# Moving the fetches of the returning tiles and the bias loads in the queue of an attention stage

## The chip, the cores and the metric

The kernel runs on one core of one Trainium2 chip. The metric is the device time of one launch in microseconds. The time before is the median of three runs, 2206.3 us (2204.29 to 2207.11). Engines are called as in the profile: PE (matrix), DVE (vector), ACT (scalar), POOL (GpSimd), SP (the engine that here only issues DMAs); PEld is the loading of PE's stationary operand.

## The reference

One layer of a decoder on 512 tokens of width 2048: RMSNorm, an attention mixer with 16 heads of width 128 in 4 key/value groups, a residual add, RMSNorm, a SwiGLU FFN with 5632 hidden columns, a residual add and a last RMSNorm. The mixer has three branches, and their outputs are added with gates computed from the tokens:

```python
s_c = q . kcc + bias_c          # 31 compressed key blocks
s_s = q . ks  + bias_s          # selected blocks; with 512 tokens all 8 blocks are selected
s_w = q . kw  + bias_w          # sliding window of 512
o = gates[0] * softmax(s_c) @ vcc + gates[1] * softmax(s_s) @ vs + gates[2] * softmax(s_w) @ vw
h = x + o @ w_out
```

Each softmax is causal, and the bias depends on the distance of query and key. Everything is float32.

## The kernel before, in words

Matmuls are done three times on split operands: a float32 matrix is kept as a high part (rounded) and a low part (the rest), and `three` adds high x high, high x low and low x high in PSUM (L267, L268 and L269). Splitting costs one ACT instruction (the high part) and one DVE instruction (the low part): for weights these are L97 and L98, which turn a loaded `raw` tile into `whi` and `wlo`.

The attention stage runs over heads `h`, and for each head over four blocks `t` of 128 queries (block `t` sees `t + 1` blocks of keys). The parts of its work:

- `scores(h, t)`: PE computes the scores of all three branches into one PSUM tile `sc`; DVE adds the bias (`tb`, one tile of 128 x 512 a head, in a pool of two) and finds the maximum (L791); ACT takes exponentials and their sums (L793) into the tile `P[t]`. `P[0]` and `P[2]` share memory, and so do `P[1]` and `P[3]`.
- `finish(h, t)`: DVE scales by gate over sum (L798, L799, L805) and transposes within blocks of 32 x 32 (L806); then SP issues four DMAs that write `P[t]` to DRAM, `d_p[t]` (L808). This is the way out of a tile.
- `fetch(t)`: SP issues one DMA that reads `d_p[t]` back into its place in the tile `PT` (L812, `ptr<-d_p`). With the blocks placed anew, this completes the transpose. There is one place for each `t`, so it can be written again only when the last reader of the head before is done. This is a returning tile.
- `turn(h, b, kt)`: ACT and DVE split the part of `PT` that key block `kt` of branch `b` needs (L829 and L833, into `pth` and `ptl`). The order is `kt` = 3, 2, 1, 0, each for branch 0 and 1, and last the compressed branch (`b` = -1), in which DVE writes low parts with L831. Key block 3 needs tile 3 alone, key block 2 needs tiles 2 and 3, and so on. The compressed branch reads all four places and is their last reader.
- `values(h, b, kt)`: PE multiplies with the values and adds in the PSUM tile `o` (L267 to L269; L844 for the compressed branch). `head_out` splits `o`; for heads below 12 two DMAs write it to DRAM (L855).

The order is written out by hand. A head has 12 steps. In step `i`, `turn` does part `i` and `values` does part `i - 2`; in between stand the scores of the next head (steps 2, 5, 8 and 11 for `t` = 3, 2, 1, 0) and their `finish` (steps 3, 6 and 9 for `t` = 3, 2 and 1, and step 0 of the next head for `t` = 0). After each step `pump` gives PE matmuls of other work (the projections of later heads and groups, and at the end a part of the output projection), until a running sum has reached the step's share of 20800 per head. The weights of that work are loaded by POOL (`W.queue = pool`).

All of these `L808`, `L812`, `L855` and bias DMAs are issued by SP, in program order: an issue that has to wait holds back all behind it. In heads 12 to 15 SP also issues `reload_o` (three pairs of 1 MB each from `d_o` into `hn_h` and `hn_l`, L696), and transfers of the tile `stage` (L702, L718).

The functions that the diff touches:

Of the kernel before, what the change touches and what calls it, by code (L numbers as in the profile page):

```python
# [19 lines left out]
S, D, H, DH, G, HPG = 512, 2048, 16, 128, 4, 4  # L20
# [153 lines left out]
def nsa_block(ctx: ExitStack, tc: tile.TileContext, x, rel_bias, mix_g, ffn_g, fin_g, w_in, w_out,  # L174
# [455 lines left out]
    with ExitStack() as st2:  # L630
# [105 lines left out]
        def pump(h, step):  # L736
            at = h + (step + 4) / STEPS
            goal = 20800 * min(at, 13) + 18300 * max(at - 13, 0)
            while done["ns"] < goal:
                c = next(stream, "end")  # L740
                if c == "end":
                    return
                done["ns"] += c or 0

        def drain_to(n):
            while done["n"] < n:
                c = next(stream, "end")
                if c == "end":
                    return
                done["ns"] += c or 0  # L750

        def needed(h):

            return 4 * ((h - 2) // 4) + (1 if h % 4 > 1 else 3) if h > 1 else 0
# [4 lines left out]
        def load_bias(h):  # L759
            if h < H:  # L760
                TB[h] = ap_.tile([128, S], F32, name="tb")
                (nc.sync if h else pool).dma_start(TB[h], bass.AP(tensor=d_u.tensor, offset=d_u.offset + h * UL + 127,
                                                 ap=[[H * UL - 1, 128], [1, S]]))
# [5 lines left out]
        def scores(h, t):  # L769
            g, n = h // HPG, 128 * (t + 1)  # L770
            (qh, ql), (kh, kl) = Q[h], KK[g % 2]
            if t == NT - 1:
                HS[h] = dict(
                    mx=ap_.tile([128, NT, 3], F32, name="mx"), sm=ap_.tile([128, NT, 3], F32, name="sm"))
            s = HS[h]
            at = 224 + (512 if t == 1 else 0)
            cuts = [0, 288] + [c for c in (800, 1056) if c <= 32 + 2 * n]
            if cuts[-1] < 32 + 2 * n:
                cuts.append(32 + 2 * n)
            for c0, c1 in zip(cuts, cuts[1:]):  # L780
                three(sc[:, at + c0:at + c1], qh[:, tok(t)], ql[:, tok(t)], kh[:, c0:c1], kl[:, c0:c1], True, True)
            c = CX[t][:, :NCMP]
            regions = [(c, c, c, sc[:, at:at + NCMP], biasc[:, h, 24 - 8 * t:24 - 8 * t + NCMP])]
            bt = TB[h][:, S - n:].rearrange("p (n s) -> p n s", s=128)
            sw = sc[:, at + 32:at + 32 + 2 * n].rearrange("p (n b s) -> p b n s", b=2, s=128)
            for b in range(2):
                u = ap_.tile([128, S], F32, name="u")[:, :n]
                regions.append((u.rearrange("p (n s) -> p n s", s=128), u.rearrange("p (n j s) -> p j n s", j=4, s=32),
                                branch(t, b).rearrange("p j (n s) -> p j n s", s=32), sw[:, b], bt))
            for i, (u, v, p, ps, bias) in enumerate(regions):  # L790
                dve.tensor_tensor_reduce(out=u, in0=ps, in1=bias, op0=OP.add, op1=OP.min, scale=-1.0,  # L791
                                         scalar=1e38, accum_out=s["mx"][:, t, i:i + 1])
                act(p, v, AF.Exp, bias=s["mx"][:, t, i:i + 1], scale=-1.0, accum_out=s["sm"][:, t, i:i + 1])  # L793
            s[t] = [c] + [branch(t, b) for b in range(2)]

        def finish(h, t):
            r = HS[h]["sm"][:, t]
            dve.reciprocal(r, r)  # L798
            dve.tensor_mul(r, r, gates[:, t, h])  # L799
            for i, p in enumerate(HS[h].pop(t)):  # L800
                o = p
                if not i:
                    o = P[t][:, :3, runs[t] - 32:]
                    p = CX[t].unsqueeze(1).to_broadcast([128, 3, 32])
                dve.tensor_scalar(o, p, r[:, i:i + 1], None, op0=OP.mult)  # L805
            dve.transpose(P[t], P[t])  # L806
            for i in range(4):
                nc.sync.dma_start(d_p[t][:, :, i].rearrange("j a r -> a j r"), P[t][32 * i:32 * (i + 1)])  # L808

        def fetch(t):  # L810

            nc.sync.dma_start(PT[:, :, PT_STEP * t:PT_STEP * t + runs[t]], d_p[t].rearrange("j a i r -> (j a) i r"))  # L812

        def arrived(rows, c0, t0, step):
            v = PT[:rows, :, c0:c0 + 32]
            p, i, c = v.ap
            return bass.AP(tensor=v.tensor, offset=v.offset, ap=[p, [step, NT - t0], i, c])

        def turn(h, b, kt):
            n = S - 128 * kt  # L820
            th = ap_.tile([128, 512], F32R, name="pth", bufs=3)
            tl = ap_.tile([128, 512], F32R, name="ptl")
            rows = 128 if b >= 0 else 96
            if b < 0:
                src = arrived(rows, 64, 0, PT_STEP + 64)
            else:
                src = arrived(rows, PT_STEP * kt + 32 * (kt + 1) * b + 32 * kt, kt, PT_STEP + 32 * b)
            th4, tl4 = (x[:rows, :n].rearrange("p (t i s) -> p t i s", i=4, s=32) for x in (th, tl))
            act(th4, src, AF.Copy)  # L829
            if b < 0:  # L830
                dve.tensor_tensor(th4[32:64], src[32:64], th4[32:64].bitcast(F32), op=OP.subtract)  # L831
            else:
                dve.tensor_tensor(tl4, src, th4.bitcast(F32), op=OP.subtract)  # L833
            HS[h]["t", b, kt] = th[:rows, :n], tl[:rows, :n]

        def values(h, b, kt):
            s, g = HS[h], h // HPG
            first = "o" not in s
            if first:
                s["o"] = ps2.tile([128, 512], F32, name="o", bufs=1)  # L840
            th, tl = s.pop(("t", b, kt))
            o = s["o"][:, 128 * kt:]
            if b < 0:
                mm(o, vcc[:, g], th, start=first, stop=True, skip_group_check=True)  # L844
            else:
                vh, vl = (v[:, kt, 128 * b:128 * (b + 1)] for v in VV[g % 2])
                three(o, vh, vl, th, tl, first, False)

        def head_out(h):
            o = HS[h]["o"]  # L850
            if h < 12:
                f = [ap_.tile([128, S], F32R, name=f"of{i}", bufs=1) for i in range(2)]
                split_from(o, *f)
                for i in range(2):
                    nc.sync.dma_start(d_o[h, i], f[i].bitcast(F32))  # L855
            else:
                split_from(o, hn_h[:, h], hn_l[:, h])
            del HS[h]

        W.queue = pool  # L860
        load_bias(0)
        for i in range(4):
            scores(0, 3 - i)
            if i:
                finish(0, 4 - i)
            if i > 1:
                fetch(5 - i)
            pump(-1, 8 + i)
        for h in range(H):
            seq = [(b, kt) for kt in (3, 2, 1, 0) for b in (0, 1)] + [(-1, 0)]  # L870
            for i in range(STEPS):
                if i == 0:
                    load_bias(h + 1)
                if i in (1, 3):
                    fetch((3 - i) // 2)
                if i < 9:
                    turn(h, *seq[i])
                if i == 0:
                    finish(h, 0)
                if h + 1 < H:  # L880
                    if i == 2:
                        drain_to(needed(h + 1))
                    if i % 3 == 2:
                        scores(h + 1, 3 - i // 3)
                    elif i % 3 == 0 and i:
                        finish(h + 1, 4 - i // 3)
                    if i in (9, 10):
                        fetch(12 - i)
                if 2 <= i < 11:
                    if i == 2 and h % HPG == 0:  # L890
                        drain_to(h)
                    values(h, *seq[i - 2])
                    if i == 10:
                        head_out(h)
                pump(h, i)
# [592 lines left out]
```

## Time and profile before

| | |
|---|---|
| median of three runs | 2206.3 us |
| profiled execution | 2204.51 us |
| its span | 2202.8 us, mean granted clock 0.989 |
| PE busy | 2124.8 us (96%) |
| DVE busy | 1636.1 us (74%) |
| ACT busy | 926.8 us (42%) |
| POOL busy | 118.1 us (5%) |
| SP's DMA queue (q1) | 42.2% of 16 DMA engines, 289.68 MB |
| landing of a `ptr<-d_p` fetch, from issue | 2.7 / 4.9 / 9.7 us (least, median, most) |

The profile is one execution; times are from the start of its span. A row in order of time has start, length, engine, line, operation, output and inputs, shape and count; the bracket tells how long the engine had been idle before, and what ended that. A row of waits has the total, the number and the longest wait. An `SPq` row that joins several issues tells the time from the first to the last.

### The profile page before, as it was taken

To read this page: it belongs to the slowest core of one execution; us is meant where nothing else is said; L and a number is where in the kernel's file an instruction comes from. 1 tells how busy PE (TensorE), PEld (TensorE's weight loads), DVE (VectorE), ACT (ScalarE), POOL (GpSimd) and SP (SyncE) were. 2 spreads that over 40 slices of the span, in tenths; PEclk is the share of its full clock that TensorE was granted. 3 is DMA by queue.
4 is the path that set the end of the run, shared out by engine and by line. 5 is a ranking of instruction groups with operands and counts; after the bars stand their busy time and mean duration, and the time that the engine had idled before them with its cause. 6 is when DMAs were issued, how large, how long until landed. Compare 5 with 4: busy or idle time off the path is not lost.

```text
span 2202.8 us, 37129 instructions
## 1 busy us (share of the span) xinstructions
PE 2124.8 (96%) x14697; PEld 1960.2 (89%) x14697; DVE 1636.1 (74%) x2680; ACT 926.8 (42%) x1433; POOL 118.1 (5%) x195
## 2 busy tenths in 40 slices
PE   9999889898988999999999999999999999999998
PEld 7898777787778888999999999999999988989996
DVE  5565767676666536798888888888888788877785
ACT  5343444444444423444344443434343444444343
POOL 1000111111100000000000000000000000001000
PEclk9999999999999999999999999999999999999999
DMA  7555666666577563343444433333333585878894
GB/s 226 185 148 148 175 169 179 175 165 184 156 235 250 167 224 130 96 139 124 131 125 125 134 119 122 125 127 123 125 125 125 209 318 181 300 275 303 309 336 148
DMA packets 279147, 394.37 MB, mean 179 GB/s; under 512 B 34763, under 2 KB 208891, under 8 KB 278332
## 3 DMA queue, kind: packets, MB, share of 16 engines
q1 hardware_dynamic: 255324, 289.68, 42.2%
q0 software_dynamic: 21744, 98.12, 12.7%
q10 hardware_dynamic: 1904, 4.20, 0.5%
q8 instruction: 115, 1.88, 0.4%
q14 instruction: 60, 0.49, 0.1%
HBM read 323.67 MB, written 73.50 MB: 180 GB/s over the span
## 4 chain that ended last, share of the span: by engine, by line
PE 65%; DMA 3%; DVE 3%; ACT 2%; issue 1%; SPq 1%; POOL 0%; ACTq 0%; DVEq 0%; POOLq 0%
PE f L269 18%; PE f L268 18%; PE f L267 18%; DMA ptr<-d_p 2%; PE proj L267 1%; PE proj L268 1%; PE proj L269 1%; PE pp L267 1%; PE pp L269 1%; PE pp L268 1%; PE po L268 1%; PE po L269 1%; PE po L267 1%; DMA al<-d_s 1%; SPq L808 1%
## 5 line engine op out<-in xcount | busy, mean ns | idle before, releaser
L98 DVE TENSOR_TENSOR wlo<-raw,whi 128x1024 fp32r<-128x1024 f32 (+1 forms) x226 | 270.7, 1200 | 114.9 <-ACT whi L97 114.6
L97 ACT ACTIVATE whi<-raw 128x1024 fp32r<-128x1024 f32 (+1 forms) x226 | 234.3, 1040 | 227.4 <-DVE raw L987 123.2
L987 DVE TENSOR_TENSOR tlo<-tt,thi 128x1536 fp32r<-128x1536 f32 (+2 forms) x135 | 197.2, 1460 | 109.0 <-ACT thi L1089 88.8
L267 PE MATMUL f<-hn_h,whi 128*128 128x256 f32 x984 | 272.3, 277 | 0.8 <-ACT E L1047 0.8
L269 PE MATMUL f<-hn_h,wlo 128*128 128x256 f32 x984 | 272.2, 277 | 0.0
L268 PE MATMUL f<-hn_l,whi 128*128 128x256 f32 x984 | 272.2, 277 | 0.0
L1084 ACT ACTIVATE whi<-raw 128x1024 fp32r<-128x1024 f32 x123 | 126.0, 1057 | 292.3 <-DVE raw L987 282.1
L267 PE MATMUL proj<-hn_h,whi 128*128 128x512 f32 x512 | 207.5, 405 | 0.5 <-ACT hn_h L402 0.5
L268 PE MATMUL proj<-hn_l,whi 128*128 128x512 f32 x512 | 204.4, 399 | 0.3 <-DVE hn_l L403 0.3
L269 PE MATMUL proj<-hn_h,wlo 128*128 128x512 f32 x512 | 204.5, 400 | 0.0
L267 PEld LDWEIGHTS f<-hn_h,whi 128*128 128x128 f32 x984 | 184.9, 188 | 1.2 <-ACT E L1047 1.2
L269 PEld LDWEIGHTS f<-hn_h,wlo 128*128 128x128 f32 x984 | 184.9, 188 | 0.0
L268 PEld LDWEIGHTS f<-hn_l,whi 128*128 128x128 f32 x984 | 184.9, 188 | 0.0
L833 DVE TENSOR_TENSOR ptl<-ptr,pth 128x128 fp32r<-128x128 f32 (+3 forms) x128 | 59.9, 486 | 138.9 <-ACT pth L829 135.0
L1089 ACT ACTIVATE thi<-tt 128x1536 fp32r<-128x1536 f32 x82 | 121.8, 1486 | 84.6 <-PE f L268 75.1
L267 PE MATMUL proj<-whi,hn_h 128*128 128x256 f32 (+2 forms) x496 | 147.4, 297 | 0.0
L987 DVE TENSOR_TENSOR wlo<-raw,whi 128x1024 fp32r<-128x1024 f32 x123 | 147.1, 1223 | 0.0
L269 PE MATMUL proj<-whi,hn_l 128*128 128x256 f32 (+2 forms) x496 | 146.6, 296 | 0.0
L268 PE MATMUL proj<-wlo,hn_h 128*128 128x256 f32 (+2 forms) x496 | 146.4, 295 | 0.0
L269 PE MATMUL f<-whi,tlo 128*128 128x512 f32 x320 | 125.1, 391 | 0.6 <-DVE tlo L987 0.6
L268 PE MATMUL f<-wlo,thi 128*128 128x512 f32 x320 | 125.2, 391 | 0.0
L267 PE MATMUL f<-whi,thi 128*128 128x512 f32 x320 | 124.9, 390 | 0.0
(323 smaller groups left out, 6149.3 us busy)
## 6 DMA issues: line engine op xcount, KB each, us to landing
raw<-in_ffn_w_in SPq DMA_DIRECT2D x135, 512.0 KB, 3.7
raw<-in_ffn_w_out SPq DMA_DIRECT2D x88, 512.0 KB, 6.0
rawx<-in_ffn_w_in SPq DMA_DIRECT2D x41, 512.0 KB, 4.9
rawx<-d_a SPq DMA_DIRECT2D x31, 512.0 KB, 4.9
ah<-d_s POOLq DMA_DIRECT2D x16, 896.0 KB, 7.4
al<-d_s POOLq DMA_DIRECT2D x16, 896.0 KB, 9.8
raw<-in_nsa_w_in SPq DMA_DIRECT2D x24, 512.0 KB, 4.7
raw<-in_nsa_w_in POOLq DMA_DIRECT2D x24, 512.0 KB, 4.5
```

The source lines that it names most:

```text
L97: self.nc.scalar.activation(hi[:, :n], src, AF.Copy)
L98: self.nc.vector.tensor_tensor(lo[:, :n], src, hi[:, :n].bitcast(F32), op=OP.subtract)
L267: mm(o, ah, bh, start=start, stop=False, skip_group_check=True)
L268: mm(o, ah, bl, start=False, stop=False, skip_group_check=True)
L269: mm(o, al, bh, start=False, stop=stop, skip_group_check=True)
L808: nc.sync.dma_start(d_p[t][:, :, i].rearrange("j a r -> a j r"), P[t][32 * i:32 * (i + 1)])
L833: dve.tensor_tensor(tl4, src, th4.bitcast(F32), op=OP.subtract)
L987: dve.tensor_tensor(o, a, b, op=OP.subtract)
L1084: act(h, r, AF.Copy)
L1089: act(h, ttf, AF.Copy)
```

## The change

The fetches of tiles 3 and 2 for head `h + 1` move from steps 9 and 10 of head `h`, where they stood behind `finish(h + 1, 1)`, to step 8, right behind the `turn` of the compressed branch. The fetch of tile 1 moves from step 1 to step 0, ahead of `finish(h, 0)`; that of tile 0 stays in step 3. The bias of a head is loaded in step 4, two heads ahead, in place of step 0 of the head before it; the bias of head 1 is loaded ahead of the loop. In the prologue, ahead of head 0, `pump` is given the goals of steps 9, 10, 11 and 11.7 in place of 8, 9, 10 and 11. No instruction is added or taken away.

```diff
         W.queue = pool
         load_bias(0)
+        load_bias(1)
         for i in range(4):
             scores(0, 3 - i)
             if i:
                 finish(0, 4 - i)
             if i > 1:
                 fetch(5 - i)
-            pump(-1, 8 + i)
+            pump(-1, min(9 + i, 11.7))
         for h in range(H):
             seq = [(b, kt) for kt in (3, 2, 1, 0) for b in (0, 1)] + [(-1, 0)]
             for i in range(STEPS):
-                if i == 0:
-                    load_bias(h + 1)
-                if i in (1, 3):
-                    fetch((3 - i) // 2)
+                if i == 4:
+                    load_bias(h + 2)
+                if i in (0, 3):
+                    fetch(1 - i // 3)
                 if i < 9:
                     turn(h, *seq[i])
+                if i == 8 and h + 1 < H:
+                    fetch(3)
+                    fetch(2)
                 if i == 0:
                     finish(h, 0)
                 if h + 1 < H:
@@ -884,8 +888,6 @@
                         scores(h + 1, 3 - i // 3)
                     elif i % 3 == 0 and i:
                         finish(h + 1, 4 - i // 3)
-                    if i in (9, 10):
-                        fetch(12 - i)
                 if 2 <= i < 11:
                     if i == 2 and h % HPG == 0:
                         drain_to(h)
```

## The prediction

> **What bounds the kernel now.** I read the stage rows first, then the waits, then one head boundary in order of time. Columns of the stage view: stretch, length, busy time of PE, PEld, DVE, ACT and POOL, granted clock, DMA share, GB/s. The attention stage runs from about 205 to 770; its stretches here begin at the first DVE subtraction of a head, and 222.14 to 642.08 are heads 0 to 11.
>
> ```profile
> 222.14:642.08 419.94, 379.65 (x2028) 322.92 (x2028) 287.86 (x792) 187.94 (x493) 52.24 (x70) 0.97 0.63 173
> 257.70:292.83 35.13, 30.83 (x145) 25.14 (x145) 24.17 (x66) 15.77 (x43) 4.48 (x6) 1.00 0.63 172
> 642.08:681.37 39.29, 32.05 (x175) 27.52 (x175) 24.18 (x66) 15.44 (x41) 3.00 (x4) 0.91 0.93 317
> 681.37:714.75 33.38, 28.66 (x217) 26.89 (x217) 22.70 (x64) 14.30 (x39) 2.99 (x4) 0.99 0.72 219
> 714.75:747.96 33.21, 29.54 (x214) 28.87 (x214) 21.86 (x63) 13.59 (x38) 2.21 (x3) 0.91 0.59 177
> 747.96:770.00 22.04, 20.91 (x150) 20.04 (x151) 11.16 (x22) 8.06 (x14) 2.14 (x3) 0.92 0.51 153
> 770.00:2202.80 1432.80, 1420.95 (x10759) 1350.53 (x10757) 1139.66 (x1470) 592.74 (x670) 42.44 (x79) 1.00 0.52 177
> ```
>
> After 770, PE is busy 99% of the time, so time saved in the attention stage comes off the end. Inside the stage PE idles 40.3 us in heads 0 to 11 (419.94 less 379.65) and 16.8 us in heads 12 to 15 (7.24 + 4.72 + 3.67 + 1.13). The waits between 205 and 765 say for whom:
>
> ```profile
> ACT pth L829 <- DMA ptr<-d_p: 115.5, 45, 7.4
> PE o L267 <- ACT pth L829: 36.7, 17, 4.1
> PE o L268 <- DVE ptl L833: 11.2, 16, 1.0
> PE o L844 <- DVE pth L831: 8.8, 9, 1.1
> ```
>
> A chain is seen here: DMA (the returning tiles, `ptr<-d_p`), then ACT, then DVE, then PE. One head in order of time shows how it closes on itself:
>
> ```profile
> 257.72 0.33 PE L267 MATMUL o<-pth,v0h 128*128 128x128 f32 x1 [2.11 <-ACT pth L829]
> 259.01 0.58 DVE L806 STREAM_TRANSPOSE p<-p 128x384 f32<-128x384 f32 x1
> 260.96 0.33 PE L268 MATMUL o<-ptl,v0h 128*128 128x128 f32 x1 [0.97 <-DVE ptl L833]
> 266.73 0.94 ACT L829 ACTIVATE pth<-ptr 128x384 fp32r<-128x384 f32 x2 [1.81 <-DMA ptr<-d_p]
> 280.08 0.68 DVE L831 TENSOR_TENSOR pth<-ptr,pth 32x512 fp32r<-32x512 f32 x1
> 280.81 0.50 PE L844 MATMUL o<-pth,vcc 96*128 96x512 f32 x1 [1.14 <-DVE pth L831]
> 284.98 0.84 DVE L806 STREAM_TRANSPOSE p<-p 128x640 f32<-128x640 f32 x1
> 285.88 1.75 SPq L808 DMA_DIRECT2D d_p<-p  x4
> 287.54 0.19 ACT L793 ACTIVATION_READ_ACCUMULATOR p<-u,mx 128x1 f32 x1
> 287.68 1.20 SPq L812 DMA_DIRECT2D ptr<-d_p  x2
> 292.49 0.31 ACT L829 ACTIVATE pth<-ptr 128x128 fp32r<-128x128 f32 x1 [4.76 <-DMA ptr<-d_p]
> 292.83 0.29 DVE L833 TENSOR_TENSOR ptl<-ptr,pth 128x128 fp32r<-128x128 f32 x1 [5.90 <-ACT pth L829]
> 292.85 0.33 PE L267 MATMUL o<-pth,v0h 128*128 128x128 f32 x1 [2.18 <-ACT pth L829]
> ```
>
> The tiles' place in PT is free at 280.76, when L831 ends. The fetch leaves only at 287.68, because in SP's order it stands behind the way out of another tile (L808), which waits for the transpose that ends at 285.82. It is needed at once: ACT stands idle 4.76 us, DVE 5.90, PE 2.18. So the period of 35.13 is a loop of DVE, SP and DMA: 23.06 us from DVE's first subtraction (257.70) to the end of L831, 6.9 until the fetch leaves, and 5.15 until DVE subtracts again. PE's own work in this head is 30.83.
>
> The stalls also cost clock:
>
> ```profile
> 222.65:226.05 3.40, 3.40 (x11) 2.82 (x12) 2.80 (x8) 1.02 (x3) 0.61 (x1) 0.50 0.80 249
> 290.91:294.32 3.41, 1.47 (x7) 1.20 (x8) 1.39 (x7) 1.46 (x3) 0.00 (x0) 1.00 1.02 308
> 294.33:301.15 6.82, 6.42 (x19) 4.94 (x18) 5.38 (x17) 3.61 (x9) 1.49 (x2) 0.50 0.76 200
> 574.23:581.04 6.81, 6.24 (x19) 4.88 (x18) 5.38 (x17) 3.26 (x9) 1.49 (x2) 0.50 0.79 201
> 656.15:662.96 6.81, 5.75 (x14) 4.58 (x15) 4.24 (x15) 4.64 (x11) 0.00 (x0) 0.50 1.06 392
> 748.31:751.71 3.40, 3.40 (x16) 3.40 (x17) 3.30 (x10) 2.33 (x5) 0.34 (x1) 0.50 0.14 30
> ```
>
> The stall that ended at 292.85 left PE busy only 1.47 us of 3.41, and the next 6.82 us were granted at half speed, which loses half of them. Heads 0 to 11 hold four such stretches, the first and the last of them shown with the one at 294.33, 23.8 us together (11.9 lost); heads 12 to 15 hold three, 17.0 us (8.5 lost), of which the first and the last are shown. The most that can be gained is therefore 40.3 + 11.9 = 52.2 in heads 0 to 11, and 16.8 + 8.5 = 25.3 after them: 77.5 us.
>
> **The change, part by part.** No instruction is added or removed; DMAs move in SP's queue, with no change in number or size.
>
> Fetches of tiles 3 and 2, moved ahead of the four L808 issues of tile 1. They now wait for L831 and leave at about 281 (L808 leaves 0.06 us after its transpose, so 0.3 is ample). Landing is bounded by the rows of the same line:
>
> ```profile
> ptr<-d_p SPq DMA_DIRECT2D x16, 576.0 KB, 4.7
> DMA to landing us min/median/max: 2.7/4.9/9.7
> hn_l<-d_o SPq DMA_DIRECT2D x3, 1024.0 KB, 9.9
> ```
>
> I take 4.7, the median of tile 3's own transfers: it lands at 285.8. ACT is then not free: its last accumulator read ends at 287.73. What is late next is therefore ACT's exponentials. DVE starts 0.34 us after ACT does (292.49 to 292.83), at 288.07 in place of 292.83. The DVE loop becomes 23.06 + 7.31 = 30.37 against PE's 30.83: PE becomes the bound, with half a microsecond to spare. PE's inner stalls have to be checked against that. From its first `values` matmul to L844, PE needs 280.81 − 257.72 − 0.97 − 1.14 = 20.98, DVE 23.06; so DVE must enter a head 2.1 us ahead. In the rest of the head PE needs 292.85 − 280.81 − 2.18 = 9.86 and DVE 7.31, which gives it 2.55 ahead. So L844 and the L268 stall go too, but narrowly, and I leave 0.2 us per head. Head 1 can stand for the twelve: their mean DVE time is 24.0 against its 24.17, their mean PE work (379.65 − 11.9) / 12 = 30.6 against 30.83. Head 0 starts without the lead and keeps 1.1 at L844, and it keeps the 1.7 lost at 222.65. Gain: 52.2 − 2.4 − 2.8 = 47.0.
>
> The queues the two fetches pass: behind them on SP wait the L808 issues, ready at 285.82, while the fetches occupy SP for 1.2 us after 281. That costs nothing with 3.5 us to spare. POOL's queue, the weights, is not touched, but its loads now overlap with the fetches; that is a rival below.
>
> Fetch of tile 1, moved before the last tile's way out, and the bias load, moved from step 0 to step 4 of the head before. Tile 1 then leaves once its own way out has landed. That was issued by 287.63; with 2 us for a small transfer (an estimate, below the 2.7 minimum of the fetches) it is about 289.6. The way out of tile 0 stands behind it and is ready 1.9 us after DVE's first subtraction (257.70 to 259.59), at 290.0, so it loses nothing. ACT uses tile 1 9 us after DVE starts the head (266.73, where it now waits 1.81 for it), at 297.1, and the fetch has 7.5 us for that: this wait goes too. I cost both moves at nothing; the cover is these 7.5 us, and without it ACT would wait the landing time of 4.9 there. The bias is read at step 2 and now lies there a head earlier.
>
> Heads 12 to 15, where the queue holds reloads and stage transfers as well:
>
> ```profile
> 657.21 0.69 PE L267 MATMUL o<-pth,v1h 128*128 128x384 f32 x1 [4.06 <-ACT pth L829]
> 665.75 0.40 SPq L696 DMA_DIRECT2D hn_h<-d_o  x1
> 669.01 0.68 DVE L831 TENSOR_TENSOR pth<-ptr,pth 32x512 fp32r<-32x512 f32 x1
> 705.03 0.39 SPq L702 DMA_DIRECT2D stage<-in_x  x1
> 707.59 1.23 SPq L812 DMA_DIRECT2D ptr<-d_p  x2
> 714.77 0.48 PE L267 MATMUL o<-pth,v1h 128*128 128x128 f32 x1 [3.77 <-ACT pth L829]
> ```
>
> The 4.06 goes, since tile 1 is now ahead of the reload. But tile 3 of the next head stands behind the last reload, which lands some 10 us after 665.75; that is 1.5 us later than ACT could use it. Head 12 then runs at DVE's 30.4 + 1.5 against PE's 28.6 (32.05 less 3.4): 3.3 stay. Before head 14, tile 3 leaves 2 us earlier only, behind the stage load: of 3.77, 1.5 stay. Head 14: DVE's loop, scaled by its busy time, is 30.4 − 2.3 = 28.1 against 26.4 of PE work: 1.7 stay. Gain: 25.3 − 6.5 = 18.8.
>
> Prologue: `pump` gives one step's weight matmuls earlier. The code counts them at 0.65 us a group, and one step (20.8 / 12 = 1.73) makes three groups, 2 us. They stand ahead of the second block of scores, whose start may come up to 2 us later, or not at all where PE had been waiting there. Head 0 waits for its first tile in any case. I take a loss of 0.4, nearer to no change; the bounds are a gain of 1.7 (the half speed at 222.65 goes) and a loss of 2.
>
> Sum: 47.0 + 18.8 − 0.4 = 65.4. The profiled execution took 2204.5 (span 2202.8), so 2139.1; the median of the three runs stands 1.8 higher, so I predict **2141 us**.
>
> The half speed after a stall of 2.2 us is a row of this trace. The Trainium skill, "TensorE: Matmul & The Clock Gate", section "HAM oscillation — how this bites in real kernels", states the abstract rule as "no PE-idle gaps >~3.4µs"; by it stalls of 2 us do not bring the half speed of heads 1 to 11, their removal does not return its 10.2 us, and the sum would be 2151. The trace row disagrees: half speed followed a window with 1.94 us of idling.
>
> **The rivals.**
>
> The fetch lands late and DVE stays the bound. At 281 a 512 KB weight load is often under way, which at 287.68 had ended. For it: the 9.7 us maximum of the line. With that, the loop is 23.06 + 10.34 = 33.4, 2.6 above PE's work, 31 us in twelve heads: 2172 us. Against it: the median is 4.9 with such overlaps already in it, and landing may take 6.7 before DVE is late at all. The Trainium skill, "DMA: Bandwidth & Descriptors", section "Issuing engines are not separate DMA queues", says that DMAs from different engines run on the same 16 engines and interleave; that speaks for this rival, and the trace has no row of this fetch beside such a load.
>
> The half-speed stretches stay: 294.33 and 574.23 are 280 us apart, eight heads, with one more halfway. If they follow the load of the chip and not the stall, their 20.4 us lose 10.2 again: 2151 us. Against it: the first follows a stall at once, and after 770, with PE at 99%, the clock is 1.00.
>
> The change does not free the fetch: something else holds it until about 287, for example the landing of an earlier transfer. Then the loop is as long as before: 2206 us. Against it: at 280 the transfers before it on SP are long landed.
>
> Slower, by the order of SP's queue: the two fetches hold SP, and the way out of tile 1, with all that follows it, comes late. The slack is 3.5 us; each microsecond beyond costs some 15 us over the heads. The 65 us gained would be eaten at about 8 us of holding; at 9 us the time would be about 2217. Against it: two issues take 1.2 us, and they wait for a DVE instruction that precedes the transpose in DVE's own order.
>
> **How the numbers follow.** PE-bound heads (2128 to 2155): 0.58. Late landing, DVE-bound (2155 to 2185): 0.20. Half speed stays (about 2151): 0.06. A new wait takes most (2185 to 2202): 0.05. Nothing freed: 0.03. Slower: 0.08. The range goes from 2128 (all 77.5 us gained) to 2172 (landing at its maximum); it holds the first and third case and most of the second. Faster by over 0.2% (4.4 us, about what a measurement of this kernel tells from no change) has 0.89, within it 0.03, slower 0.08.
>
> **What would show it.** Right: `ptr<-d_p` leaves SP right behind L831 and ahead of the four L808; ACT's wait for it falls from 115.5 to under 30; PE's waits at L267, L268 and L844 from 56.7 to about 15; the period of head 1 from 35.1 to 31; the clock in heads 1 to 11 is 1.00. Wrong: PE waits for L833 as often as now, with ACT still waiting for the DMA (late landing), or with ACT and DVE never idle (their loop is longer than I read it).

## The result, and the profile after

The changed kernel takes 2136.4 us (median of four runs, 2133.99 to 2139.59) against 2206.5 (2204.29 to 2207.11): a ratio of 0.9685, 95% interval 0.9668 to 0.9702. The profiled execution took 2137.7, its span is 2136.0, so it is 66.8 us shorter in its span than the one of before.

The stage first, in the columns of the prediction's stage view, for the changed kernel. One thing differs in how it is cut. Before, PE's first `values` matmul of a head began within 0.1 us of DVE's first subtraction (292.85 and 292.83). Now PE is 2.6 us behind DVE there, so the stretches begin at PE's matmul: heads 0 to 11, then 12, 13 and 14, two parts of what follows, and last heads 1 to 11.

```profile
222.32:587.04 364.72, 361.09 (x2028) 315.07 (x2029) 288.31 (x799) 185.07 (x494) 52.27 (x70) 1.00 0.71 201
587.04:620.01 32.97, 28.92 (x177) 25.47 (x175) 21.79 (x60) 13.93 (x38) 3.00 (x4) 1.00 1.03 361
620.01:650.66 30.65, 29.61 (x217) 28.28 (x218) 22.68 (x65) 14.07 (x39) 3.00 (x4) 0.94 0.68 203
650.66:680.14 29.48, 27.14 (x214) 26.04 (x215) 23.02 (x69) 14.39 (x40) 2.21 (x3) 1.00 0.70 212
680.14:702.00 21.86, 19.71 (x140) 18.60 (x139) 9.13 (x15) 5.38 (x10) 2.14 (x3) 0.92 0.57 173
770.00:2136.00 1366.00, 1354.65 (x10446) 1294.50 (x10444) 1114.33 (x1446) 572.87 (x650) 41.77 (x78) 1.00 0.52 175
256.06:587.04 330.98, 329.19 (x1885) 288.73 (x1884) 262.61 (x727) 169.40 (x452) 47.77 (x64) 1.00 0.71 201
```

Heads 0 to 11 do the same 2028 matmuls in 364.7 us instead of 419.9, and heads 1 to 11 run with PE idle for 1.8 us of 331 and at clock 1.00. A head takes 30.09 us (330.98 / 11). The end of the stage gained far less: head 12 still has 4 us of idle PE, with the DMA engines full, and two of the later stretches show a lower clock.

The waits between 205 and 765 (total, number, longest):

```profile
DVE ptl L833 <- ACT pth L829: 72.0, 46, 5.3
ACT pth L829 <- DMA ptr<-d_p: 22.0, 10, 7.3
PE o L267 <- ACT pth L829: 5.6, 3, 2.7
PE o L268 <- DVE ptl L833: 4.1, 2, 2.3
PE o L844 <- DVE pth L831: 2.6, 5, 1.3
```

ACT's wait for returning tiles fell from 115.5 to 22.0 us, PE's three waits from 56.7 to 12.3. One boundary between heads in order of time, that from head 1 to head 2:

```profile
275.66 0.68 DVE L831 TENSOR_TENSOR pth<-ptr,pth 32x512 fp32r<-32x512 f32 x1
276.04 1.48 POOL L81 DMA_DIRECT2D raw<-in_nsa_w_in  x2 [2.58 <-DVE wlo L98]
276.37 1.22 SPq L812 DMA_DIRECT2D ptr<-d_p  x2
280.56 0.84 DVE L806 STREAM_TRANSPOSE p<-p 128x640 f32<-128x640 f32 x1
281.49 2.04 SPq L808 DMA_DIRECT2D d_p<-p  x4
282.13 0.32 ACT L793 ACTIVATE cx<-cx,mx 128x31 f32<-128x31 f32 x1 [2.74 <-DVE mx L791]
283.13 0.19 ACT L793 ACTIVATION_READ_ACCUMULATOR p<-u,mx 128x1 f32 x1
283.22 0.29 ACT L829 ACTIVATE pth<-ptr 128x128 fp32r<-128x128 f32 x1
283.55 0.29 DVE L833 TENSOR_TENSOR ptl<-ptr,pth 128x128 fp32r<-128x128 f32 x1 [1.03 <-ACT pth L829]
286.11 0.22 PE L267 MATMUL o<-pth,v0h 128*128 128x128 f32 x1
```

The two fetches leave SP in the instant in which L831 ends, 5.1 us ahead of the way out of tile 1 that used to stand in front of them. At 283.22 ACT takes the first returning tile without a wait: what it had been doing until then are the last exponentials of the new head, which wait for DVE's maxima (L791). So the head is now closed by DVE, then ACT, then DVE; the DMA has dropped out of the loop, and PE follows 2.6 us behind with no wait at all.

### The profile page after: what moved, and what is told of

It reads as the page before. It is cut to its first block, busy times and chain, and to the rows that moved or that the text cites. A ratio compares the mean times of both kernels' runs of the same rounds, so it can differ in the third digit from the quotient of the medians.

```text
span 2136.0 us, 37198 instructions
## 1 busy us (share of the span) xinstructions
PE 2103.2 (98%) x14697; PEld 1949.5 (91%) x14697; DVE 1634.8 (77%) x2680; ACT 922.9 (43%) x1433; POOL 118.2 (6%) x195
## 4 chain that ended last, share of the span: by engine, by line
PE 87%; DVE 5%; DMA 4%; ACT 2%; issue 2%; SPq 1%; POOL 0%; ACTq 0%; DVEq 0%; POOLq 0%
PE f L268 19%; PE f L269 19%; PE f L267 19%; PE proj L267 7%; PE proj L268 6%; PE proj L269 6%; DMA d_p<-p 1%; DVE wlo L98 1%; DMA ptr<-d_p 1%; PE pp L269 1%; PE pp L268 1%; PE pp L267 1%; PE po L269 1%; PE po L267 1%; PE po L268 1%
## 5 line engine op out<-in xcount | busy, mean ns | idle before, releaser
L269 PEld LDWEIGHTS proj<-hn_h,wlo 128*128 128x128 f32 x512 | 96.5, 189 | 21.5 <-DVE wlo L98 0.2
```

The lines of the kernel that those rows point to most:

```text
L269: mm(o, al, bh, start=False, stop=stop, skip_group_check=True)
```

## The experiments

Where a row of stretches is quoted below, it covers heads 1 to 11, cut at PE's first `values` matmul of heads 1 and 12; the changed kernel's row is 330.98 us.

**The changed kernel again, beside other runs.** No edit.

> The changed kernel once more, beside the next three: 2134 to 2140.

Measured: 2137.9 us (2136.86 to 2139.89), ratio 0.9691 [0.9677, 0.9706]. The kernels below are held against 0.9685 and this; two kernels within 0.0015 of each other aren't told apart.

**Which part carries the gain.** The early fetches alone, and everything but them.

```diff
 # e1_fetch32_alone: the kernel before, with only this
+                if i == 8 and h + 1 < H:
+                    fetch(3)
+                    fetch(2)
...
-                    if i in (9, 10):
-                        fetch(12 - i)
```

> The early fetches of tiles 3 and 2 alone; bias, tile 1 and prologue as before. Theory 1 (the loop was closed by the fetch, but the old place of the bias would close it next): the bias leaves SP about 289 in the frame of head 1, lands 6 us later, and DVE wants it 3.5 us after its first subtraction, at 291.6, so each head waits some 3 us for it: period 33, time about 2172. Rival (the fetches of tiles 3 and 2 are the whole gain, the rest is without effect): within 5 us of the changed kernel, 2132 to 2142.

> All of the change but the early fetches of tiles 3 and 2, which stand behind the way out of tile 1 as before. Theory 1: the loop of head 1 stays at 35 us (DVE 23.06, 6.9 until the fetch leaves, 5 until it is used); only the 4 us before the reload in head 12 and small waits go: about 2198. Rival (bias and tile 1 were worth half of the gain by themselves): about 2170.

Measured: the early fetches alone 2148.7 us (2147.79 to 2150.68), ratio 0.9736 [0.9722, 0.9751]; the rest alone 2201.1 (2196.05 to 2201.92), 0.9967 [0.9953, 0.9981]. The first lies between the two theories. The early fetches carry some 58 us and the rest alone 6, and together they give 70: about 6 us appear only where both are made. Heads 1 to 11 of the early fetches alone, and its waits there:

```profile
255.99:594.45 338.46, 330.72 (x1885) 288.18 (x1884) 263.41 (x727) 170.37 (x452) 47.87 (x64) 1.00 0.72 197
ACT pth L829 <- DMA ptr<-d_p: 18.4, 13, 2.4
DVE u L791 <- DMA tb<-d_u: 6.6, 8, 1.4
```

DVE now waits for the bias (`tb`), 6.6 us in eight waits, which accounts for most of the 7.5 us by which these heads are longer. In the profile of before, with the bias loaded at the same step, this wait is nearly absent:

```profile
DVE u L791 <- DMA tb<-d_u: 0.8, 2, 0.5
```

There the head stood still for the late fetch, and the bias had time to land: before, one was issued at 290.11 and used from 296.40; with the early fetches alone, one was issued at 284.62 and used from 287.67, as soon as it had landed. In the changed kernel, where the bias comes a head earlier, the wait is gone. The rest alone came out near its theory 1.

**The prologue.**

```diff
-            pump(-1, min(9 + i, 11.7))
+            pump(-1, 8 + i)
```

> The changed kernel with the old goals of pump in the prologue. Theory (the earlier weight matmuls only shift a wait, 0.4 us): 2133 to 2139, no difference from the changed kernel. Rival (they fill 1.6 us of PE and spare the half speed of head 0): 2138 to 2141.

Measured: 2139.3 us (2135.24 to 2140.78), 0.9690 [0.9675, 0.9704]. The time lies in the rival's range, but the ratio to the kernel before, run beside it, is that of the changed kernel, so this part of the change can't be told from nothing. What the rival has it spare, half speed in head 0, the changed kernel still has (at 234.85, shown below).

**How much room the fetch has.** First the bias load put ahead of the early fetches:

```diff
-                if i == 4:
-                    load_bias(h + 2)
...
                 if i == 8 and h + 1 < H:
+                    load_bias(h + 2)
                     fetch(3)
```

> The changed kernel with the bias of two heads ahead issued right ahead of the early fetch of tile 3, which delays that fetch by the issue (0.5 us) and by the 256 KB ahead of it. Theory 1 (the early fetch now lands 0.3 to 1 us ahead of its use, since it shares the DMA engines with a weight load): DVE waits some 0.8 us a head, about 2146. Rival (1.9 us to spare, as the prediction worked out): no change, 2133 to 2140.

Measured: 2138.7 us (2137.2 to 2141.47), 0.9692 [0.9677, 0.9706]. This missed its aim. The bias load had nothing late to wait for, so SP issued it at 272.29, while the fetch waited for L831 and left at 276.34 as before: it was not delayed. The second attempt delays tile 3 by the fetch of tile 2 itself:

```diff
-                    fetch(3)
-                    fetch(2)
+                    fetch(2)
+                    fetch(3)
```

> The changed kernel with the two early fetches in the other order, tile 2 ahead of tile 3. Theory 1 (tile 3 lands just in time: in the changed kernel it lands about 6 us after its issue and some 0.6 us before ACT could use it): an issue of 0.6 us and 448 KB more ahead of it put its landing 1.2 to 2 us later, so the loop of each of heads 1 to 11 grows by 0.6 to 1.4 us, with ACT waiting for the DMA again at the head's start, and the time is 2144 to 2152. Rival (there are the 1.9 us to spare that the prediction took): periods stay at 30.1 and the time at 2136 to 2139.

Measured: 2151.3 us (2149.8 to 2154.33), 0.9763 [0.9748, 0.9777]. Theory 1 holds. Heads 1 to 11 and their waits, and then the landing of tile 3 (KB each, median us from issue to landing) in this kernel; the row of the changed kernel follows in a fence of its own:

```profile
255.81:594.14 338.33, 330.45 (x1886) 288.39 (x1884) 262.01 (x726) 170.25 (x452) 47.76 (x64) 1.00 0.70 197
ACT pth L829 <- DMA ptr<-d_p: 6.8, 11, 1.5
PE o L844 <- DVE pth L831: 7.6, 10, 1.2
...
ptr<-d_p SPq DMA_DIRECT2D x16, 576.0 KB, 7.0
```

```profile
ptr<-d_p SPq DMA_DIRECT2D x16, 576.0 KB, 5.7
```

Tile 3 lands 7.0 us after its issue, and that issue is some 0.6 us later: 1.9 us in all. ACT then waits for returning tiles eleven times in eleven heads, and the head grows by 0.67 us. So the changed kernel has about a microsecond to spare at that place, not 1.9. The eleven heads account for 7.4 us of the loss; heads 12 to 14 are another 6.7 us longer (99.8 us from 594.14 to 693.92, against 93.1), where ACT's waits at the start of the next head are 4.9, 5.5 and 4.1 us, against 4.0, 2.9 and none.

**What bounds a head now.** Three runs: one DVE instruction of 0.7 us more in a head, one less, and four small ones moved to ACT.

```diff
 # e5_dve_more, in turn
                 dve.tensor_tensor(tl4, src, th4.bitcast(F32), op=OP.subtract)
+                if (b, kt) == (1, 0):
+                    dve.tensor_tensor(tl4, src, th4.bitcast(F32), op=OP.subtract)
 # e6_dve_less, in turn
-                dve.tensor_tensor(th4[32:64], src[32:64], th4[32:64].bitcast(F32), op=OP.subtract)
+                pass
 # e10_cx_on_act, in finish
-                    p = CX[t].unsqueeze(1).to_broadcast([128, 3, 32])
+                    act(o, CX[t].unsqueeze(1).to_broadcast([128, 3, 32]), AF.Copy, scale=r[:, i:i + 1])
+                    continue
```

> The changed kernel with one DVE subtraction (128 x 512, 0.69 us) done twice in each head. Theory 2 (since the change DVE's loop of 30.1 us is the bound of heads 0 to 11): the period grows to 30.7 and the time by about 8 us, to 2145. Rival (PE is the bound, as the prediction said, with DVE half a microsecond below it): under 3 us more, 2136 to 2139.

> The changed kernel without the DVE subtraction L831 (0.68 us a head): the low part of the compressed branch's probabilities is left out, the high part stands in its place. Theory 2: the period falls from 30.1 until PE's own work stops it, at about 29.8, and the waits at L844 go: 3 to 5 us less, about 2132. Rival (PE is the bound): no change, 2134 to 2140.

> The changed kernel with the scaling of the compressed branch's probabilities (L805, 128 x 96, 0.29 us on DVE, four times a head) done by ACT. Theory 1 (the loop through DVE and ACT sets the period of 30.1, and PE's own work is 29.6 to 29.8): DVE has 1.1 us less in the loop, the period falls to PE's 29.6 to 29.8, and the time is 2131 to 2134. Rival (ACT is as much a part of the loop: the transpose waits for ACT's copy, and L829 and L793 stand behind it): periods stay at 30.1 or grow by some tenths, and the time is 2136 to 2141.

Measured: 2146.7 us (2144.11 to 2148.53), 0.9727 [0.9711, 0.9744]; 2132.9 (2131.7 to 2136.91), 0.9671 [0.9656, 0.9685]; and 2139.8 (2139.14 to 2144.88), 0.9715 [0.9699, 0.9732]. Heads 1 to 11 of the three, in this order:

```profile
256.81:596.64 339.83, 330.22 (x1886) 288.67 (x1884) 270.24 (x738) 169.53 (x452) 47.76 (x64) 1.00 0.70 196
```

```profile
254.23:581.24 327.01, 327.01 (x1886) 288.93 (x1884) 256.61 (x717) 169.44 (x452) 47.75 (x64) 1.00 0.72 204
```

```profile
261.24:590.93 329.69, 329.24 (x1885) 288.97 (x1884) 255.97 (x683) 185.39 (x496) 47.76 (x64) 1.00 0.71 202
```

With 0.69 us more on DVE a head grows by 0.80 (339.83 less 330.98, over 11): the loop through DVE is the bound. Without the 0.68 us of L831 (0.55 less of busy time, 262.61 to 256.61 over 11) it shrinks by 0.36 only, to 29.73, and PE is busy for all of the 327.01 us: there PE is the bound. The whole time of that kernel is only at the edge of what is told apart from the changed one; the reading rests on the row of the heads. So in the changed kernel DVE's loop (30.09) stands 0.36 us above PE's own work (29.73).

Moving the scaling to ACT has the rival right. Heads 1 to 11 gain only 1.3 us, though DVE has 6.6 us less to do: ACT belongs to the same loop, and now waits for DVE's factors (`sm`) before each copy, four times a head (total, number, longest, in the same heads):

```profile
ACT p L804 <- DVE sm L799: 39.4, 44, 1.1
```

More than that is lost ahead of head 1, where it begins 5.2 us later. PE's first `values` matmul in this kernel:

```profile
225.77 0.45 PE L267 MATMUL o<-pth,v0h 128*128 128x128 f32 x1 [4.49 <-issue]
```

In the changed kernel it begins at 222.32. What holds its heads at 29.97, a quarter of a microsecond above PE's work, isn't settled.

**The last heads.** The reloads and the stage transfers issued by POOL, and the stage transfers alone.

```diff
 # e7_reload_pool: all three; e9_stage_pool: the last two
-                nc.sync.dma_start(t[:, 4 * i:4 * i + 4].bitcast(F32),
+                pool.dma_start(t[:, 4 * i:4 * i + 4].bitcast(F32),
...
-            nc.sync.dma_start(st, x[:, c].rearrange("(t p) c -> p t c", p=128))
+            pool.dma_start(st, x[:, c].rearrange("(t p) c -> p t c", p=128))
...
-            nc.sync.dma_start(d_h[:, c].rearrange("(t p) c -> p t c", p=128), st)
+            pool.dma_start(d_h[:, c].rearrange("(t p) c -> p t c", p=128), st)
```

> The changed kernel with the three reloads and the stage transfers issued by POOL in place of SP. Theory 3 (in heads 12 to 14 the fetches still stand behind these in SP's queue, which leaves PE waits of 1.33, 2.73 and 1.04 us and 1.7 us of half speed): 4 to 7 us less, about 2131. Rival (they wait for the same DMA engines whichever queue they are in): no change, 2134 to 2140, or slower where POOL's own weight loads come late.

> The changed kernel with the transfers of the tile stage (L702 and L718) issued by POOL, the reloads staying in SP's queue. Theory 1 (in head 13 the fetch of tile 3 is late because it stands behind the stage load in SP's order): the fetch leaves right behind L831, the period of head 13 falls from 30.6 by 2 to 3 us, and the time is about 2134. Rival (the transfers share the 16 engines, so that the order on SP is not what counts, as moving the reloads showed): the heads' sum stays and the time is 2136 to 2139.

Measured: 2139.9 us (2136.92 to 2142.49), 0.9699 [0.9684, 0.9714], and 2135.2 (2133.87 to 2136.1), 0.9687 [0.9673, 0.9702]. Neither can be told from the changed kernel. Heads 12 and 13 of the first, and then of the second, with the issues that matter:

```profile
587.19:626.97 39.78, 31.75 (x178) 27.23 (x176) 23.10 (x65) 15.03 (x40) 6.72 (x9) 0.91 0.88 304
626.97:655.19 28.22, 27.95 (x220) 26.66 (x218) 23.23 (x67) 13.65 (x38) 4.51 (x6) 1.00 0.74 215
...
601.73 0.69 PE L267 MATMUL o<-pth,v1h 128*128 128x384 f32 x1 [5.00 <-ACT pth L829]
```

```profile
587.59:622.87 35.28, 29.06 (x177) 25.46 (x175) 21.83 (x60) 13.92 (x38) 3.74 (x5) 1.00 0.99 350
622.87:652.34 29.47, 29.47 (x218) 28.30 (x218) 24.40 (x71) 14.54 (x40) 4.51 (x6) 0.94 0.71 204
...
610.07 3.71 SPq L812 DMA_DIRECT2D ptr<-d_p  x2
610.48 0.75 POOL L702 DMA_DIRECT2D stage<-in_x  x1
```

Head 13 gains in both (30.65 to 28.22 and 29.47), and head 12 gives it back (32.97 to 39.78 and 35.28). With the reloads on POOL, the fetch of tile 1 runs beside them and PE stands still 5.00 us for it in the middle of head 12. With the stage transfers on POOL, the first of them is issued 0.4 us after the fetch of tile 3 and lies beside it. The shares of 0.88 to 1.03 for the 16 DMA engines in head 12 suggest why the order helps little: hardly any transfer time is free there to move a tile into. The Trainium skill, "DMA: Bandwidth & Descriptors", section "Issuing engines are not separate DMA queues", says that transfers run on the same 16 engines whichever engine issued them; these two runs agree.

**Both edits of the last two groups.** `e9` and `e10` in one kernel.

> The changed kernel with both edits: the stage transfers issued by POOL, and the scaling of the compressed branch's probabilities done by ACT. If theory 1 of both holds, the gains add, since they lie in different heads: about 2130. If only one holds, 2132 to 2134. If neither does, 2136 to 2141.

Measured: 2138.6 us (2137.53 to 2139.87), 0.9704 [0.9689, 0.9718]: neither theory of gain held, and no version was found that is measurably faster than the changed kernel and leaves nothing out.

## Why the prediction was right, and where it was not

The forecast of 2141 us was 4.6 above the median. Its sum held better than its terms: two of them were off by 7 to 8 us, in opposite directions, and that these nearly cancel is luck. The measured terms are those of the two profiled executions, with the stretches quoted.

| term of the sum | predicted gain | measured |
|---|---|---|
| prologue | -0.4 | -0.2 (222.14 to 222.32) |
| heads 0 to 11 | 47.0 | 55.2 (419.94 less 364.72) |
| heads 12 to 14 and what follows | 18.8 | 11.8 (6.3 + 2.7 + 3.7 - 1.0) |
| sum | 65.4 | 66.8 |

**The chain, and what the move does: right.** The fetch left right behind L831, the ACT wait fell under 30 us, PE's waits to 12.3 (about 15 predicted), head 1 to 30.1 (31 predicted), the clock in heads 1 to 11 was 1.00. The way out of tile 1 was issued with its transpose as before: the rival in which SP is held had no effect.

**Heads 0 to 11: the cap was too low.** The step that failed is "The most that can be gained is therefore 40.3 + 11.9", which took PE's busy time for PE's work. Without the half speed (11.9 before, 1.7 after, from one stretch in head 0 shown below), the same 2028 matmuls were counted as 367.8 us busy before and as 359.4 after. The 8.4 us between them are, within 0.2, what this term was short by. At least part of them lies in matmuls behind a wait, which last longer in the trace. The first matmul of a head takes 0.33 us at 292.85 in before, where PE waited for it, and 0.22 at 286.11 now, where it doesn't. The matmul of the compressed branch (busy time, mean ns of one; then the idle time of PE ahead of it), in heads 1 to 11 of before, of the changed kernel and of the one without L831:

```profile
L844 PE MATMUL o<-pth,vcc 96*128 96x512 f32 x11 | 5.5, 500 | 7.8 <-DVE pth L831 7.7
L844 PE MATMUL o<-pth,vcc 96*128 96x512 f32 x11 | 5.2, 471 | 1.8 <-DVE pth L831 1.3
L844 PE MATMUL o<-pth,vcc 96*128 96x512 f32 x11 | 4.3, 395 | 0.0
```

So the busy time of before held time that went with the stalls; that all of the 8.4 us is of this kind is a reading, not shown. What the prediction left standing in these heads, 5.2 us, was right: 3.6 of idling and 1.7 of half speed.

**"PE becomes the bound, with half a microsecond to spare": wrong in order.** DVE's loop was forecast at 30.37 and measured at 30.09; PE's work was put at 30.83 (30.6 in the mean) by the same over-reading and is 29.73 where it never waits. So DVE's loop with ACT is still the bound, 0.36 us above PE, as the run with more and the run with less DVE work show. That the two lie so close is why the period came out right to within a microsecond.

**The landing: 4.7 us taken, 5.7 measured.** It lies beside weight loads of POOL (276.04 in the boundary above); that these are the cause of the longer landing was not tested. The 1.9 us to spare were about one. The late-landing rival did not come about, but it was nearer than the text had it: swapping the two fetches was enough to bring it, and cost 13 to 17 us, by the times and by the ratios.

**"I cost both moves at nothing": they carry a part of the gain.** Against the kernel with the early fetches alone, the places of the bias, of tile 1 and the prologue are worth 10 to 12 us; the bias and tile 1 were not run apart. For tile 1 the prediction did let two waits go (1.81 and 4.06); for the bias it only said that it would lie there earlier. The wait for the bias that the early fetches alone would have brought, up to 1.4 us a head, is the one that it did not see, because in the trace of before another wait covered all but 0.8 us of it.

**Heads 12 to 15: 6.5 us were to stay, about 13 did.** Idling is 4.1, 1.0, 2.3 and 2.2 in the four stretches shown above, 9.6 in all, and two half-speed stretches lost 3.4. The first was foreseen by its mechanism (tile 3 behind the last reload) and only larger. In head 15 tile 1 came late, which the prediction had not listed; it had left no half speed there either, though it left stalls standing of the kind that it had seen bring it.

**The half speed: the trace row held.** Three pairs of neighbouring stretches of 3.4 us of the changed kernel:

```profile
217.79:221.20 3.41, 1.98 (x11) 1.38 (x9) 2.29 (x9) 2.05 (x7) 0.00 (x0) 1.00 0.79 237
221.20:224.61 3.41, 2.29 (x12) 1.83 (x12) 3.06 (x9) 0.51 (x2) 1.51 (x2) 1.00 0.71 162
231.45:234.85 3.40, 1.56 (x8) 1.09 (x7) 3.40 (x7) 0.03 (x1) 0.80 (x2) 1.00 0.58 135
234.85:238.25 3.40, 3.40 (x10) 2.62 (x9) 1.90 (x8) 3.34 (x9) 0.69 (x1) 0.50 0.94 276
688.82:692.23 3.41, 1.69 (x10) 1.44 (x11) 1.03 (x2) 0.94 (x2) 0.00 (x0) 1.00 0.26 60
692.23:695.63 3.40, 3.40 (x17) 3.40 (x16) 1.29 (x2) 2.04 (x4) 0.00 (x0) 0.50 0.61 200
```

Half speed followed where PE had been busy for 1.56 and 1.69 of 3.4 us, and with the stalls out of heads 1 to 11 it is out of them too. It did not follow every such stretch: in head 14 of the same execution PE waited 2.26 us and was busy for 1.63, and clock 1.00 followed:

```profile
661.51:664.92 3.41, 1.63 (x12) 1.63 (x13) 3.41 (x11) 1.01 (x4) 0.76 (x1) 1.00 1.02 271
664.92:668.33 3.41, 3.41 (x28) 3.32 (x27) 2.48 (x8) 2.27 (x7) 0.00 (x0) 1.00 0.80 279
```

The Trainium skill, "TensorE: Matmul & The Clock Gate", section "HAM oscillation — how this bites in real kernels", gives the rule as no idle gap over about 3.4 us; the two stretches with 1.84 and 1.72 us of idling that half speed followed differ from it, as did the row of before. The rival built on that rule, 2151 us, did not occur.

## What to carry to other kernels

When a queue is in order, put what waits for the earliest event first, and ask of each transfer moved how much time it has from issue to use: here two fetches that leave when L831 ends, and not 6.9 us later, were worth 58 us, though the first then had only about a microsecond to spare, and the order of the two was worth 13 to 17. After a stall is closed, look for the waits it had been covering (here the bias), since the trace of before hardly shows them. And read PE's work from a stretch in which it never waits: its busy time in a stretch full of stalls was 2% too high, which hid that another engine was the bound.

## What was unexpected in the hardware

The same stall cost clock in one execution of a kernel and not in another. In the prologue of the changed kernel PE waited 2.51 us ahead of 222.32, longer than the stall of 1.84 ahead of 234.26; but it was spread over two neighbouring stretches of 3.4 us (1.98 and 2.29 us busy, the first two rows of the pairs above) and clock 1.00 followed, while the shorter one lay in one stretch and half speed followed. In the profiled execution of the same kernel taken again (`e0_after_again`) PE waited 2.56 us at the same place, ahead of 222.28. There nearly all of the wait lay in one stretch, and 6.8 us of half speed followed:

```profile
218.54:221.95 3.41, 1.18 (x8) 0.84 (x6) 2.39 (x5) 1.90 (x6) 0.00 (x0) 1.00 0.81 228
221.95:225.37 3.42, 3.09 (x9) 2.61 (x10) 2.19 (x9) 0.43 (x2) 1.51 (x2) 0.50 0.79 221
225.37:228.78 3.41, 3.41 (x11) 2.83 (x10) 1.76 (x7) 2.35 (x8) 0.00 (x0) 0.50 0.87 233
```

So where a stall falls counts, and not only its length. How idle a stretch has to be isn't settled: 1.69 us busy brought half speed in one case, 1.63 did not in another. These are a few cases of two executions, and none was varied in an experiment.
